# A gate table in pieces of 64 tokens, read for two expert groups at once, with its loads and the gelu loads at later places and the rows spread otherwise

## The chip, the core and the metric

The kernel runs on one core of a Trainium2 chip. The metric is the time of the whole program on the device in microseconds (us). Three runs of the kernel before took 2616.76 to 2627.11 us, with a median of 2618.74 us.

## What is computed

Two transformer blocks follow each other on 512 tokens of width 1024. The change touches the middle of the first block, a product-key expert layer with 16384 experts. Every token picks 16 experts for each of 8 heads, and an expert adds gate × gelu(down row · token) × up row:

```python
def peer_ffn(x, w_query, keys_1, keys_2, expert_down, expert_up):
    q = (x @ w_query).astype(f32).reshape(b, s, PEER_HEADS, 2, PEER_HALF)
    s1 = jnp.einsum("bshc,hkc->bshk", q[..., 0, :], keys_1)
    s2 = jnp.einsum("bshc,hkc->bshk", q[..., 1, :], keys_2)
    v1, i1 = lax.top_k(s1, PEER_TOPK)
    v2, i2 = lax.top_k(s2, PEER_TOPK)
    ...
    top_score, pos = lax.top_k(cand_score, PEER_TOPK)
    experts = jnp.take_along_axis(cand_idx, pos, axis=-1)
    gates = jax.nn.softmax(top_score, axis=-1)
    ...
        u = jnp.take(expert_down, ei, axis=0)
        act = jax.nn.gelu(jnp.einsum("btd,bthkd->bthk", xi, u), approximate=False)
        vv = jnp.take(expert_up, ei, axis=0)
        return jnp.einsum("bthk,bthkd->btd", gi * act, vv)
```

The numbers are float32; the kernel splits each factor of a large product into a high and a low half-precision part and multiplies three times.

## The kernel before

**Two ways for the experts.** The last 384 tokens (`TD`) go through all experts densely: the gelu of every expert for every token is formed and multiplied by a gate that is zero for experts that were not picked. The 16384 experts are 32 groups of 512, two groups make a pair `q` (16 pairs). The first 128 tokens are done row by row: 128 steps fetch one row of the down table for each token with an indirect DMA from GpSimd (`fetch`, 0.5 MB a step, a ring of 4 buffers), VectorE multiplies it with the token and sums (`row_step`, L1003), and 128 further steps do the same with the up table (L1015).

**Weights.** All weights stream through one list, 1 MB each. The SP queue loads a weight into one of 4 `raw` buffers (L304), ScalarE squares and sums it (`junk`, L319), TensorE adds that over the partitions (`ps_ss`, L206), VectorE and GpSimd make a power-of-two scale of it (`mi`, `scw`, L208 to L211), and ScalarE and VectorE split the weight into its high part (L333) and its low part (L334). Loads run three weights ahead of the one in use, the square and the sum three ahead, the split one ahead. A `raw` buffer is free after the split of its weight. All of it is in program order on each engine, so a `ps_ss` on TensorE that waits for a late load stops the matmuls behind it, though they don't need that weight yet.

**Stage 1** (about 700 to 1225 us of the trace) forms the gelu of the first 20 groups (`R1`), stores it in DRAM (`gedram`), selects the experts of the tokens (`select`), and writes the gate table into DRAM (`gdram`). `gate_chunk` makes the gates of 32 tokens: VectorE builds one-hot rows (`ohA`, `ohB`, `ohL`, `ohH`), TensorE multiplies them (`ps_g`), ScalarE copies the result into two staging tiles `stg`, one for each half of the experts, and issues their two writes of 1 MB. The pool has 3 `stg` buffers. `PLAN` orders the 12 chunks g0 to g11, the selections s1 to s3 and the down groups D.

**Stage 2** (about 1225 to 2083 us) runs over the pairs in the list `order` (0, 10, 1, 11, 2, 3, 12, 4, 5, 13, 6, 14, 7, 8, 15, 9). The list `stage2` holds its steps: `L` loads a pair's gelu back (two loads of 768 KB, 3 buffers), `D` forms a quarter of the gelu of a pair that has none yet, `C` (`combine`) multiplies gelu by gates (L1200) and splits the product into `cexp` (L1201 on ScalarE, L1202 on VectorE), and `U` multiplies a quarter of the pair's up weights with it (`ps_u`; 2 output tiles of 24 matmuls each, added into `hT` at L1223). `load_gates` reads the gates of one group, 768 KB in 12 runs of 512 bytes for each partition, into one of 2 `gt` buffers; it is called from `C` for the pair after. The quarters D of a later pair lie between the quarters U of an earlier one, so stretches with D alternate with stretches that have U alone and load stored gelu (the L stretches below: 1364 to 1444, 1520 to 1604, 1684 to 1744, 1797 to 1869 and 1950 to 2018 us).

**Rows.** `tick(n)` stands after each down or up tile and moves the row count on by n: `TK` holds n for a down tile in stage 2, an up tile beside down work, an up tile without it, a late and an early down tile of stage 1. What is left is done at the end of stage 2 in `rows_done`, before the last pair.

A scheduler merges these lists into one order for each engine and queue; the order is fixed when the program is built.

## Time and profile before

| | before |
|---|---|
| median of 3 runs | 2618.74 us |
| profiled execution, its own time | 2618.21 us |
| its span in the trace | 2616.3 us |
| TensorE busy | 2312.8 us (88%) |
| VectorE busy | 1820.9 us (70%) |
| ScalarE busy | 1352.1 us (52%) |
| GpSimd busy | 805.2 us (31%) |
| moved by DMA | 453.45 MB, mean 173 GB/s |

The page gives busy times of the whole span; what an edit is worth is read from the stretch in which it lies. A matmul is pipelined, so the mean duration of one is about twice the spacing at which they start, and the spacing is what counts. "PEclk" is the granted share of TensorE's full clock: 1.00 is 2.4 GHz and 0.50 is 1.2 GHz. The DMA share is the mean busy share of the 16 DMA engines.

### The profile page before, as it was taken

How to read it: one execution, taken by the hardware profiler on the slowest of the kernel's cores; microseconds unless marked ns; L12 is line 12 of the kernel's file. 1: busy time of each engine (PE TensorE's matmuls, PEld its weight loads, DVE VectorE, ACT ScalarE, POOL GpSimd, SP SyncE). 2: the span in 40 equal slices, each digit the busy share in tenths (PEclk: the TensorE clock that was granted, in tenths of full speed). 3: DMA queues.
4: the chain of work that ended last, by engine and by line, in shares of the span. 5: the costliest groups of instructions: out<-in, count | busy, mean ns of one | idle time of the engine just before them, and what ended most of it. 6: DMA issues, size and time to landing. Idle time of an engine off the chain costs nothing.

```text
span 2616.3 us, 37153 instructions
## 1 busy us (share of the span) xinstructions
PE 2312.8 (88%) x14242; PEld 1375.9 (53%) x14242; DVE 1820.9 (70%) x3865; ACT 1352.1 (52%) x1738; POOL 805.2 (31%) x782
## 2 busy tenths in 40 slices
PE   6999999989999988977797987979897769999997
PEld 2337896334655555644453554545454556555545
DVE  6877554386657798976786877788776853766555
ACT  6453223574655567766453634545453545454543
POOL 0002444020102344723564463657565420000000
PEclk9999999999999999988898998999998979999999
DMA  4220002342244547758988787788877724100121
GB/s 187 81 81 33 1 1 101 145 165 94 83 149 175 199 160 268 257 202 299 292 312 293 258 313 273 265 301 309 285 282 262 268 82 145 65 17 33 65 97 33
DMA packets 133075, 453.45 MB, mean 173 GB/s; under 512 B 9761, under 2 KB 61473, under 8 KB 102689
## 3 DMA queue, kind: packets, MB, share of 16 engines
q1 hardware_dynamic: 85872, 272.79, 30.2%
q0 software_dynamic: 36864, 134.23, 14.3%
q10 hardware_dynamic: 10160, 44.05, 4.3%
q8 instruction: 112, 1.84, 0.3%
q14 instruction: 67, 0.54, 0.1%
HBM read 408.05 MB, written 42.99 MB: 172 GB/s over the span
## 4 chain that ended last, share of the span: by engine, by line
PE 41%; DVE 24%; DMA 16%; ACT 9%; issue 7%; POOL 3%; ACTq 0%; POOLq 0%; DVEq 0%; SPq 0%
DVE sp L334 5%; PE ps_in L372 4%; PE ps_in L373 4%; PE ps_in L374 4%; DMA ring<-in_up_rows_dram,rowi 4%; DMA raw<-in_up_dram 3%; DMA ring<-in_down_rows_dram,rowi 3%; ACT junk L319 3%; ACT sp L333 2%; DMA raw<-in_down_dram 2%; PE ps_d L374 2%; DVE usp L334 2%; PE ps_d L373 2%; PE ps_d L372 2%; PE ps_r L572 2%
## 5 line engine op out<-in xcount | busy, mean ns | idle before, releaser
L319 ACT ACTIVATE junk<-raw 128x2048 bf16<-128x2048 f32 (+1 forms) x202 | 382.9, 1896 | 418.4 <-DMA raw<-in_up_dram 244.8
L334 DVE SCALAR_TENSOR_TENSOR sp<-raw,scw,sp 128x2048 f16<-128x2048 f32 (+2 forms) x140 | 326.6, 2333 | 122.2 <-ACT sp L333 122.1
L374 PE MATMUL ps_d<-xn,sp 128*128 128x384 f16 x1024 | 341.8, 336 | 39.0 <-DVE sp L334 39.0
L374 PEld LDWEIGHTS <-sp 128*128 128x128 f16 (+1 forms) x2320 | 230.8, 100 | 249.3 <-DVE sp L334 45.3
L372 PE MATMUL ps_d<-xn,sp 128*128 128x384 f16 x1024 | 344.0, 336 | 12.6 <-ACT sp L333 8.0
L374 PE MATMUL ps_u<-cexp,usp 128*128 128x384 f16 (+2 forms) x1024 | 340.6, 333 | 8.2 <-DVE usp L334 8.2
L372 PEld LDWEIGHTS <-sp 128*128 128x128 f16 (+1 forms) x2320 | 231.1, 100 | 215.3 <-issue 31.7
L373 PE MATMUL ps_d<-xn,sp 128*128 128x384 f16 x1024 | 343.7, 336 | 0.0
L373 PE MATMUL ps_u<-cexp,usp 128*128 128x384 bf16 (+2 forms) x1024 | 341.1, 334 | 2.7 <-DVE cexp L1202 2.7
L372 PE MATMUL ps_u<-cexp,usp 128*128 128x384 f16 (+2 forms) x1024 | 340.6, 334 | 2.7 <-ACT usp L333 2.7
L373 PEld LDWEIGHTS <-sp 128*128 128x128 f16 (+1 forms) x2320 | 230.9, 100 | 209.3 <-issue 39.9
L333 ACT ACTIVATE sp<-raw,scw 128x2048 f16<-128x2048 f32 (+2 forms) x140 | 276.9, 1980 | 74.5 <-DVE scw L210 31.6
L372 PE MATMUL ps_in<-xn,sp 128*128 128x512 f16 (+2 forms) x728 | 274.2, 378 | 5.8 <-DVE cv L499 3.3
L374 PE MATMUL ps_in<-xn,sp 128*128 128x512 f16 (+2 forms) x728 | 274.2, 378 | 0.4 <-DVE sp L334 0.4
L373 PE MATMUL ps_in<-xn,sp 128*128 128x512 f16 (+2 forms) x728 | 274.2, 378 | 0.0
L996 POOL DMA_INDIRECT ring<-in_down_rows_dram,rowi x128 | 186.0, 1453 | 233.1 <-DVE ring L1003 141.7
L996 POOL DMA_INDIRECT ring<-in_up_rows_dram,rowi x128 | 201.7, 1576 | 165.4 <-DVE ysum L1015 103.7
L1015 DVE SCALAR_TENSOR_TENSOR ysum<-ring,rowg,ysum 128x1024 f32<-128x1024 f32 x127 | 162.5, 1280 | 44.2 <-DMA ring<-in_up_rows_dram,rowi 43.8
L211 POOL TENSOR_SCALAR scw<-mi 128x1 int32<-128x1 int32 x136 | 81.5, 599 | 350.9 <-DVE mi L208 325.9
L1003 DVE SCALAR_TENSOR_TENSOR ring<-ring,xrow 128x1024 f32<-128x1024 f32 x128 | 155.3, 1220 | 40.4 <-DMA ring<-in_down_rows_dram,rowi 40.4
L333 ACT ACTIVATE usp<-raw,scw 128x2048 f16<-128x2048 f32 x62 | 123.8, 1997 | 98.8 <-PE ps_u L374 85.8
L206 PE MATMUL ps_ss<-ss,ones_b 128*128 128x1 bf16 x202 | 34.1, 169 | 147.8 <-ACT junk L319 89.3
(444 smaller groups left out, 4323.2 us busy)
## 6 DMA issues: line engine op xcount, KB each, us to landing
raw<-in_down_dram SPq DMA_DIRECT2D x64, 1024.0 KB, 5.4
raw<-in_up_dram SPq DMA_DIRECT2D x64, 1024.0 KB, 6.7
raw<-in_w_in_dram SPq DMA_DIRECT2D x45, 1024.0 KB, 4.8
gdram<-stg ACTq DMA_DIRECT2D x24, 1024.0 KB, 7.4
gt<-gdram SPq DMA_DIRECT2D x30, 768.0 KB, 9.2
gedram<-gelu ACTq DMA_DIRECT2D x20, 768.0 KB, 5.1
gelu<-gedram SPq DMA_DIRECT2D x20, 768.0 KB, 8.5
raw<-in_w_ada_dram SPq DMA_DIRECT2D x12, 1024.0 KB, 4.8
```

The costliest lines, as they stand in the source:

```text
L206: T.matmul(ps, ones_b, sb[:, 2 * u + 1:2 * u + 2], start=(u == 0), stop=(u == n - 1))
L211: side[0].tensor_scalar(sc[:, 1:2], mi, 1.0, float(50 << 23), op0=ALU.mult, op1=ALU.add)
L319: act(junk[:, :e["n"]], e["raw"][:, :e["n"]], AF.Square, accum_out=ss[:, j:j + 1])
L333: act(sp[:, 0, :n], e["raw"][:, :n], AF.Copy, scale=e["s"])
L334: rq["lo"] = V.scalar_tensor_tensor(sp[:, 1, :n], e["raw"][:, :n], e["s"], sp[:, 0, :n], op0=ALU.mult, op1=ALU.subtract)
L372: T.matmul(ps, wh, xh, start=start, stop=False)
L373: T.matmul(ps, wh, xl, start=False, stop=False)
L374: T.matmul(ps, wl, xh, start=False, stop=stop)
L572: T.matmul(pr[:, R4(r)], Tm[:, R4(r)], x[:, R4(r)], start=True, stop=True)
L996: G.indirect_dma_start(out=r, out_offset=None, in_=src, in_offset=bass.IndirectOffsetOnAxis(ap=rowi[s % P // 64][:, s % 64:s % 64 + 1], ax ...
L1003: V.scalar_tensor_tensor(r, r, 1.0, xrow, op0=ALU.mult, op1=ALU.mult, accum_out=rowu[:, s:s + 1])
L1015: V.scalar_tensor_tensor(ysum[0], r, g, ysum[0], op0=ALU.mult, op1=ALU.add)
```

## The change

Five edits:

- The gate table is written and read in pieces of 64 tokens (`TC`) and no longer 32. Two calls of `gate_chunk` fill one pair of `stg` tiles, which is written once, as 2 × 2 MB. There are 2 `stg` buffers of 16 KB a partition where there were 3 of 8 KB, and 10 slabs where there were 14. `select` takes one `stg` buffer for its three work tiles where it took three.
- `load_gates` reads the gates of a pair at once: 1.5 MB in 6 runs of 2 KB for each partition, into a single `gt` buffer of the size of the former two.
- In the list `stage2`, C of the next pair stands behind the first U of a pair (before: ahead of it), the gate load of the pair after it (`G`, a step of its own) behind the second U, and the gelu load behind the third. At the start, two of the four D quarters of the second pair stand behind the first C.
- `TK` changes from (1.9, 1.1, 0.9, 0.5, 0.8) to (2.0, 1.15, 0.95, 0.2, 1.0).
- gelu tiles have the layout of 6 × 4 × 64 where they had 12 × 4 × 32; the instructions on them keep their element counts.

```diff
-TK = (1.9, 1.1, 0.9, 0.5, 0.8)
+TK = (2.0, 1.15, 0.95, 0.2, 1.0)
...
-    stage2 = [("L", order[0])] + ([("L", order[1])] if early_(order[1]) else halves_(order[1])) + [("C", order[0])]
+    x = [("L", order[1])] if early_(order[1]) else halves_(order[1])
+    stage2 = [("L", order[0])] + x[:2] + [("C", order[0]), ("G", order[1])] + x[2:]
     for i, q in enumerate(order):
-        if i + 1 < 16:
-            stage2.append(("C", order[i + 1]))
-        if i + 2 < 16 and early_(order[i + 2]):
-            stage2.append(("L", order[i + 2]))
+        extra = [[("C", order[i + 1])] if i < 15 else [], [("G", order[i + 2])] if i < 14 else [],
+                 [("L", order[i + 2])] if i < 14 and early_(order[i + 2]) else [], []]
         for u in range(4):
-            stage2 += [("U", q, u)] + slots[i][u]
+            stage2 += [("U", q, u)] + extra[u] + slots[i][u]
...
     def gate_chunk(ch):
-        stg = [s1.tile([P, 64, 32], F32, tag="stg", name="stg", bufs=3) for _ in range(2)]
+        if ch % 2 == 0:
+            stg_[:] = [s1.tile([P, 64, TC], F32, tag="stg", name="stg", bufs=2) for _ in range(2)]
+        stg = stg_
...
-        for hf in range(2):
-            nc.scalar.dma_start(gd[ch, hf].rearrange("p i t -> p (i t)"), stg[hf].rearrange("p i t -> p (i t)"))
+        for hf in range(2 * (ch % 2)):
+            nc.scalar.dma_start(gd[ch // 2, hf].rearrange("p i t -> p (i t)"), stg[hf].rearrange("p i t -> p (i t)"))
...
-    def load_gates(g, q=nc.sync):
-        gt = pools["2"].tile([P, TD // 32, 4, 32], F32, tag="gt", name="gt", bufs=2)
-        hf, o = divmod(g * 4, 64)
-        q.dma_start(gt.rearrange("p c i t -> p c (i t)"), gd[:, hf, :, o:o + 4, :].rearrange("c p i t -> p c (i t)"))
-        gts[g] = gt
+    def load_gates(q, eng=nc.sync):
+        gt = pools["2"].tile([P, TD // TC, 8, TC], F32, tag="gt", name="gt", bufs=1)
+        hf, o = divmod(q * 8, 64)
+        eng.dma_start(gt.rearrange("p c i t -> p c (i t)"), gd[:, hf, :, o:o + 8, :].rearrange("c p i t -> p c (i t)"))
+        gts[q] = gt
```

How the scheduler's order moves is shown at four places. First ScalarE's order at the seam between the chunks g9 and g10 in stage 1. Before:

```order
L1143 COPY stg<-ps_g 128x4x64 x15
L1146 DMA gdram<-stg 128x2048 x2
L1143 COPY stg<-ps_g 128x4x64 x16
L1146 DMA gdram<-stg 128x2048 x2
L984 ACTIVATE gelu<-ps_d,dsc 128x12x32 x2
```

And now:

```order
L1151 DMA gdram<-stg 128x4096 x2
L1148 COPY stg<-ps_g 128x4x64 x4
L984 ACTIVATE gelu<-ps_d,dsc 128x6x64 x2
L1148 COPY stg<-ps_g 128x4x64 x4
L319 ACTIVATE junk,ss<-raw 128x2048
L1148 COPY stg<-ps_g 128x4x64 x8
```

The write ahead of the copies is twice as large, the copies behind it need both of its buffers, and the next write stands 32 copies on where it stood 16 on.

Second, ScalarE's order at the end of stage 1, from the last gate write on. Before:

```order
L1146 DMA gdram<-stg 128x2048 x2
L319 ACTIVATE junk,ss<-raw 128x2048
L1187 DMA gt<-gdram 128x12x128 x2
L333 ACTIVATE sp<-raw,scw 128x2048
L319 ACTIVATE junk,ss<-raw 128x2048
```

And now:

```order
L1151 DMA gdram<-stg 128x4096 x2
L333 ACTIVATE sp<-raw,scw 128x2048
L1192 DMA gt<-gdram 128x6x512
L319 ACTIVATE junk,ss<-raw 128x2048
L984 ACTIVATE gelu<-ps_d,dsc 128x6x64 x2
```

A split has moved ahead of the first gate load and a square behind it.

Third, VectorE's order at the same place, around the first two gate products (L1200 before, L1205 now). Before:

```order
L1194 TENSOR_REDUCE ca<-cs 128x1
L1200 SCALAR_TENSOR_TENSOR gelu<-gt,ca,gelu 128x1536 x2
L334 SCALAR_TENSOR_TENSOR sp<-raw,scw,sp 128x2048
L208 TENSOR_SCALAR mi<-ps_ss 128x1
L1003 SCALAR_TENSOR_TENSOR ring,rowu<-ring,xrow 128x1024
```

And now:

```order
L334 SCALAR_TENSOR_TENSOR sp<-raw,scw,sp 128x2048
L1003 SCALAR_TENSOR_TENSOR ring,rowu<-ring,xrow 128x1024 x4
L209 TENSOR_SCALAR mi<-ps_ss 128x1
L1205 SCALAR_TENSOR_TENSOR gelu<-gt,ca,gelu 128x1536
L211 TENSOR_SCALAR scw<-mi 128x1
L1205 SCALAR_TENSOR_TENSOR gelu<-gt,ca,gelu 128x1536
L334 SCALAR_TENSOR_TENSOR sp<-raw,scw,sp 128x2048
```

One split of a down weight and four row steps now stand ahead of the gate products.

Fourth, the SP queue in the second of the L stretches (each row is a load; 768 KB for a `gelu`, 768 KB for a `gt` before and 1.5 MB now, 1 MB for a `raw`). Before:

```order
L1187 DMA gt<-gdram 128x12x128
L1181 DMA gelu<-gedram 128x1536
L304 DMA raw<-in_up_dram 128x2048
L1187 DMA gt<-gdram 128x12x128
L1181 DMA gelu<-gedram 128x1536
L304 DMA raw<-in_up_dram 128x2048
L1187 DMA gt<-gdram 128x12x128 x2
L1181 DMA gelu<-gedram 128x1536
L304 DMA raw<-in_up_dram 128x2048
L1187 DMA gt<-gdram 128x12x128
```

And now:

```order
L1186 DMA gelu<-gedram 128x1536
L304 DMA raw<-in_up_dram 128x2048
L1186 DMA gelu<-gedram 128x1536
L304 DMA raw<-in_up_dram 128x2048
L1192 DMA gt<-gdram 128x6x512
L1186 DMA gelu<-gedram 128x1536
L304 DMA raw<-in_up_dram 128x2048
L1192 DMA gt<-gdram 128x6x512
L304 DMA raw<-in_up_dram 128x2048 x2
```

Ahead of the first two `raw` loads one load has gone, and gates come later in the stretch.

On VectorE, the gate products of this stretch stand so. Before, both groups of a pair together behind their preloaded gates:

```order
L1200 SCALAR_TENSOR_TENSOR gelu<-gt,ca,gelu 128x1536
L208 TENSOR_SCALAR mi<-ps_ss 128x1
L1200 SCALAR_TENSOR_TENSOR gelu<-gt,ca,gelu 128x1536
L210 TENSOR_SCALAR scw<-mi 128x1
L1223 SCALAR_TENSOR_TENSOR hT<-ps_u,yd,hT 128x384
```

And now, with the last product of one pair first and the first product of the next pair, for which the single `gt` buffer is loaded in between, nine rows on:

```order
L1205 SCALAR_TENSOR_TENSOR gelu<-gt,ca,gelu 128x1536
L209 TENSOR_SCALAR mi<-ps_ss 128x1
L1198 TENSOR_REDUCE ca<-cs 128x1
L1199 TENSOR_REDUCE ca<-cs 128x1
L211 TENSOR_SCALAR scw<-mi 128x1
L1229 SCALAR_TENSOR_TENSOR hT<-ps_u,yd,hT 128x384
L1003 SCALAR_TENSOR_TENSOR ring,rowu<-ring,xrow 128x1024
L1208 TENSOR_TENSOR cexp<-gelu,cexp 128x6x4x64
L1229 SCALAR_TENSOR_TENSOR hT<-ps_u,yd,hT 128x384
L1003 SCALAR_TENSOR_TENSOR ring,rowu<-ring,xrow 128x1024
L209 TENSOR_SCALAR mi<-ps_ss 128x1
L1205 SCALAR_TENSOR_TENSOR gelu<-gt,ca,gelu 128x1536
L334 SCALAR_TENSOR_TENSOR usp<-raw,scw,usp 128x2048
```

Two output tiles (`hT`) lie between the two gate products now, and a weight split stands right behind the second.

## Rows read from the trace of the kernel before

**Rows 1.** Busy times by stretch (us): stage 1's end, parts of stage 2; columns first.

```profile
core 0: us, PE busy (x) PEld busy (x) DVE busy (x) ACT busy (x) POOL busy (x), PEclk, DMA share, GB/s
900.00:1225.00 325.00, 281.46 (x2143) 180.39 (x2141) 284.54 (x756) 230.11 (x348) 147.06 (x130) 0.94 0.64 237
1225.00:1290.00 65.00, 31.18 (x143) 16.06 (x144) 39.24 (x56) 27.60 (x27) 31.88 (x29) 0.71 0.85 284
1364.00:1444.00 80.00, 61.62 (x347) 34.70 (x345) 55.48 (x84) 26.32 (x23) 40.00 (x38) 0.89 0.85 290
...
1950.00:2018.00 68.00, 53.44 (x298) 29.90 (x297) 51.07 (x57) 22.43 (x20) 42.07 (x38) 0.89 0.82 292
1290.00:2083.00 793.00, 686.38 (x4122) 402.73 (x4120) 608.49 (x737) 384.69 (x320) 429.10 (x398) 0.94 0.82 285
```

**Rows 2.** TensorE's waits in 1290 to 2083 us: total us, times, longest.

```profile
PE ps_ss L206 <- ACT junk L319: 54.8, 15, 10.5
PE ps_ss L206 <- DVE mi L208: 39.6, 18, 5.9
```

**Rows 3.** VectorE's waits in 1290 to 2083 us.

```profile
DVE ysum L1015 <- DMA ring<-in_up_rows_dram,rowi: 36.0, 16, 6.8
...
DVE ring L1003 <- DMA ring<-in_down_rows_dram,rowi: 28.9, 11, 4.4
...
DVE gelu L1200 <- DMA gelu<-gedram: 17.9, 5, 8.2
```

**Rows 4.** The chain that ended last, in 1416 to 1432 us: start, us, what.

```profile
1416.40 2.40 DVE usp L334
...
1418.82 10.94 DMA raw<-in_up_dram
...
1431.89 0.16 PE ps_ss L206
```

**Rows 5.** Busy by stretch: moving a gt, a gelu, weights and rows, then 2 KB runs.

```profile
1588.00:1592.00 4.00, 0.12 (x2) 0.12 (x2) 3.81 (x4) 2.00 (x2) 2.18 (x1) 0.50 0.63 175
1608.00:1612.00 4.00, 3.87 (x24) 2.22 (x23) 4.00 (x6) 3.98 (x4) 2.04 (x1) 1.00 0.58 197
...
2043.00:2048.00 5.00, 5.00 (x33) 3.01 (x31) 3.21 (x5) 1.49 (x1) 2.87 (x4) 1.00 0.81 297
...
2163.00:2170.00 7.00, 7.00 (x43) 4.08 (x42) 0.00 (x0) 3.24 (x6) 0.00 (x0) 1.00 0.93 306
```

**Rows 6.** ScalarE at the seam g9 to g10, in order of time.

```profile
1193.64 0.81 ACTq L1146 DMA_DIRECT2D gdram<-stg  x2
...
1198.70 1.96 ACT L1143 COPY stg<-ps_g 128x256 f32<-128x256 f32 x4 [3.54 <-DMA gdram<-stg]
```

**Rows 7.** The page's DMA issues: KB each, median us to landing.

```profile
gdram<-stg ACTq DMA_DIRECT2D x24, 1024.0 KB, 7.4
gt<-gdram SPq DMA_DIRECT2D x30, 768.0 KB, 9.2
```

**Rows 8.** VectorE's row steps by shape in 900 to 1225 us: busy, mean ns.

```profile
L1003 DVE SCALAR_TENSOR_TENSOR ring<-ring,xrow 128x1024 f32<-128x1024 f32 x26 | 31.7, 1220 | 0.0
```

**Rows 9.** TensorE's longest wait in 900 to 1225 us.

```profile
PE ps_d L374 <- DVE sp L334: 27.9, 9, 7.0
```

**Rows 10.** TensorE's waits in 1220 to 1290 us.

```profile
PE ps_d L374 <- DVE sp L334: 11.1, 1, 11.1
...
PE ps_d L372 <- ACT sp L333: 6.0, 1, 6.0
```

**Rows 11.** VectorE in order of time, the first gate product.

```profile
1238.41 1.82 DVE L1200 SCALAR_TENSOR_TENSOR gelu<-gt,ca,gelu 128x1536 f32<-128x1536 f32 x1 [11.71 <-DMA gt<-gdram]
```

**Rows 12.** The chain again, in 1220 to 1245 us.

```profile
1221.66 5.91 DMA gdram<-stg
...
1228.18 12.79 DMA gt<-gdram
```

**Rows 13.** Busy times at the end of stage 2, where rows alone run.

```profile
2083.00:2106.00 23.00, 1.30 (x8) 1.19 (x7) 14.62 (x22) 2.00 (x2) 8.93 (x8) 0.55 0.65 229
```

More of the change, by code (lines that the diff above doesn't have):

```diff
@@ L105 @@
 TD = 384
+TC = 64
 RING = 4
@@ L930, in tile_model @@
     s1 = stage1.enter_context(tc.tile_pool(name="stage1", bufs=1))
-    pools["s"] = stage1.enter_context(tc.tile_pool(name="slab2", bufs=14))
+    pools["s"] = stage1.enter_context(tc.tile_pool(name="slab2", bufs=10))
     keys = raw("keys").rearrange("p (j m) -> p j m", j=16)
@@ L964, in tile_model @@
     i1T, i2T, ghT, glT = (selT[:, i] for i in range(4))
-    gd = drp.tile([TD // 32, 2, P, 64, 32], F32, name="gdram")
+    gd = drp.tile([TD // TC, 2, P, 64, TC], F32, name="gdram")
     lim = [0]
@@ L972, in expert_down @@
             pool, n = (s1, 2) if g < R1 else (pools["2"], GB)
-            gelu[g] = pool.tile([P, TD // 32, 4, 32], F32, tag="gelu", name="gelu", bufs=n)
+            gelu[g] = pool.tile([P, TD // TC, 4, TC], F32, tag="gelu", name="gelu", bufs=n)
         t, e = gelu[g], need(("d", g, u))
@@ L983, in expert_down @@
             proj3(ps[:, :TD], e, c, xnd)
-            act(t[:, :, 2 * u + c], ps[:, :TD].rearrange("p (c t) -> p c t", t=32), AF.Gelu, scale=gs)
+            act(t[:, :, 2 * u + c], ps[:, :TD].rearrange("p (c t) -> p c t", t=TC), AF.Gelu, scale=gs)
             tick(TK[0] if g >= R1 else TK[3] if g >= nd else TK[4])
@@ L1086, in select @@
         p16, st, i1, i2 = (smp.tile([P, 16, nh], F16, tag=t, name=t, bufs=1) for t in ("p16", "st", "i1", "i2"))
-        ge, t1, t2 = (s1.tile([P, 64, 32], F32, tag="stg", name="stg", bufs=3).rearrange("p i t -> p (i t)")
-                      .bitcast(F16)[:, 0:256 * nh].rearrange("p (a k h) -> p a k h", a=16, k=16) for _ in range(3))
+        tmp = s1.tile([P, 64, TC], F32, tag="stg", name="stg", bufs=2).rearrange("p i t -> p (i t)").bitcast(F16)
+        ge, t1, t2 = (tmp[:, i * 256 * nh:(i + 1) * 256 * nh].rearrange("p (a k h) -> p a k h", a=16, k=16)
+                      for i in range(3))
         each = lambda t: t[:, None].to_broadcast([P, 16, 16, nh])
@@ L1121, in select @@
         V.scalar_tensor_tensor(glT[:, sl], ps[:, 0:P], GSC, ghT[:, sl], op0=ALU.mult, op1=ALU.subtract)
+    stg_ = []
     def gate_chunk(ch):
-        stg = [s1.tile([P, 64, 32], F32, tag="stg", name="stg", bufs=3) for _ in range(2)]
+        if ch % 2 == 0:
+            stg_[:] = [s1.tile([P, 64, TC], F32, tag="stg", name="stg", bufs=2) for _ in range(2)]
+        stg = stg_
         for o8 in range(4):
@@ L1140, in gate_chunk @@
                     T.matmul(ps[:, r * P:(r + 1) * P], B[:, q, :, e2], Al[:, q, :, e2], start=False, stop=True)
-                tl_ = o8 * 8 + q4 * 4
+                tl_ = ch % 2 * 32 + o8 * 8 + q4 * 4
                 for hf in range(2):
@@ L1179, in load_gelu @@
     def load_gelu(g):
-        t = pools["2"].tile([P, TD // 32, 4, 32], F32, tag="gelu", name="gelu", bufs=GB)
+        t = pools["2"].tile([P, TD // TC, 4, TC], F32, tag="gelu", name="gelu", bufs=GB)
         nc.sync.dma_start(t.rearrange("p c i t -> p (c i t)"), ged[g])
         gelu[g] = t
-    def load_gates(g, q=nc.sync):
-        gt = pools["2"].tile([P, TD // 32, 4, 32], F32, tag="gt", name="gt", bufs=2)
-        hf, o = divmod(g * 4, 64)
-        q.dma_start(gt.rearrange("p c i t -> p c (i t)"), gd[:, hf, :, o:o + 4, :].rearrange("c p i t -> p c (i t)"))
-        gts[g] = gt
+    def load_gates(q, eng=nc.sync):
[3 more added lines that the diff above has]
+        gts[q] = gt
     def combine(*gs):
@@ L1196, in combine @@
         for g in gs:
-            t, gt = gelu.pop(g), gts.pop(g)
+            t, gt = (v.rearrange("p c i t -> p c (i t)") for v in (gelu.pop(g), gts[g // 2][:, :, g % 2 * 4:g % 2 * 4 + 4]))
             ct = pools["2"].tile([P, 2, 4, TD], F16, tag="cexp", name="cexp", bufs=4)
-            hi, lo = (v.rearrange("p i (c t) -> p c i t", t=32) for v in (ct[:, 0], ct[:, 1].bitcast(BF16)))
+            hi, lo = (v.rearrange("p i (c t) -> p c i t", t=TC) for v in (ct[:, 0], ct[:, 1].bitcast(BF16)))
             V.scalar_tensor_tensor(t, gt, ca[:, 0:1], t, op0=ALU.mult, op1=ALU.mult)
+            t = t.rearrange("p c (i t) -> p c i t", i=4)
             nc.scalar.copy(hi, t)
@@ L1241, in tile_model @@
     pools["s"] = None
-    nU, lg = 0, [g for q in order for g in (2 * q, 2 * q + 1)]
-    for g in lg[:2]:
-        load_gates(g, nc.scalar)
+    load_gates(order[0], nc.scalar)
     lim[0] = 2 * P
@@ L1253, in tile_model @@
             combine(2 * x[1], 2 * x[1] + 1)
-            nU += 2
-            for g in lg[nU:nU + 2]:
-                load_gates(g)
+        elif x[0] == "G":
+            load_gates(x[1])
         elif x[1] != order[15]:
```

## The prediction

> **What bounds the kernel now.** I read the busy times by stretch first, then the waits of the engines in the stretches with idle, then the chain. In stage 1 TensorE is busy 281 of 325 us, and VectorE 285. In stage 2 the picture changes: the start (1225 to 1290) has TensorE busy 31 of 65 us, and the body (1290 to 2083) 686 of 793, with the DMA engines at a share of 0.82 [rows 1]. The 107 us of idle in the body are not spread evenly. The five stretches that load stored gelu (L stretches, 364 us in all, the first and the last shown) hold 77 of them, 21% of their time, at DMA shares of 0.82 to 0.91; the other 429 us hold 29, 7% [rows 1]. There TensorE stands at a `ps_ss` either because ScalarE's square came late, which waits for a weight to land (54.8 us), or because VectorE had not yet emptied the sum before it (39.6 us) [rows 2]. VectorE in turn stood waiting for rows (64.9 us) and for a stored gelu (17.9 us) [rows 3]. The chain shows how it hangs together: VectorE's split frees a buffer, the weight is issued at 1418.8 us and needs 10.9 us to land, and the `ps_ss` starts 2 us after that [rows 4]. So the body is bound by TensorE where DMA has room, and by DMA and by what stands in whose queue in the L stretches. Idle costs a little more than its own length: TensorE's granted clock is 0.89 over the two L stretches shown and 0.71 at the start, a mix of its levels 1.00 and 0.50 (2.4 and 1.2 GHz) [rows 1].
>
> **The change part by part.**
>
> *Longer runs in the gate loads.* Without company, a gate load moved 175 GB/s at a DMA share of 0.63, 278 GB/s for a full share; a gelu load 197 at 0.58, 340; weights and a row 297 at 0.81, 367; loads in runs of 2 KB 306 at 0.93, 329 [rows 5]. The 32 gate loads of 768 KB are 25.2 MB: 90.5 us of all DMA engines at 278 GB/s, 76.5 at 329. That gives back 14 us of DMA time, with ends of 0 (if 2 KB runs behave as 512-byte ones) and 22 (if as whole rows, at 367). This bears on a rule: the Trainium skill, "DMA: Bandwidth & Descriptors", section Specifications, puts the minimum transfer for line rate at 512 B. By it the old runs are already at full rate and the 14 us would be 0; the rates above disagree.
>
> *Rows moved.* By `TK`, stage 1 loses 52 late tiles × 0.3 and gains 16 early ones × 0.2: 12.4 row steps fewer. Stage 2 gains 48 down tiles × 0.1 and 120 up tiles × 0.05, 10.8 steps; 17.6 in place of 16 are left for the end. In stage 2 these 10.8 × 0.52 MB at 350 GB/s are 16 us of DMA time. So the two edits cancel over all of stage 2; in the L stretches, which have some 24 of the 32 gate loads and 4 of the new rows, they leave −10.5 + 6 = −4.5 us.
>
> *Stage 1.* The pieces hold the same bytes, but a write is 4 MB in place of 2 and no spare `stg` buffer is left. Copies stand right behind a write at g9 to g10, where ScalarE waited 3.5 us for the former write [rows 6]. One write of 1 MB landed after 7.4 us [rows 7], so I take that much more: 11 us. TensorE has 46 down and 32 gate matmuls before it needs ScalarE again, about 9 us less what has run by then: +7 us on the path, bounds 0 and 11. At g1 to g2 and g5 to g6 gelu activations at TensorE's pace stand ahead of the copies and cover most of the longer write: +1 us each. Selections still wait for one written buffer, as before. Against it, 11 to 12 row steps of 1.22 us leave VectorE [rows 8], 14 us, in a part where TensorE waits 27.9 us for VectorE's splits [rows 9]; VectorE is on the path a part of the time only, so −4, bounds 0 and −14. Sum +5.
>
> *Start of stage 2.* TensorE lost 6.0 us while ScalarE, waiting to issue the first gate load, could not split, and 11.1 us because VectorE, which had waited 11.7 us for the gates, held the next split behind them [rows 10, 11]. The write took 5.9 us and the load 12.8 [rows 12]. Now the write is twice as long (+5, if another 2 MB take about the 5.9 us of these), and the load, one in place of two, shorter by 2 to 4, so the gates come no sooner. But a split and four row steps of VectorE now stand ahead of the gate product, and the first product is needed after two quarters D, not four. Of the 17 us I take 10 back, bounds 0 (the longer write holds ScalarE longer, and D runs dry) and −17.
>
> *Body.* The L stretches: −4.5 us of DMA time, as above. The queue: at the second L stretch, two loads stood ahead of each of the first two weights, and one stands there now; gates come a weight or two later, and one more load falls into the stretch with D, which has room. A load of 0.79 MB at 340 GB/s is 2.3 us; two weights in each of five stretches, half of it on the path: −11. Stored gelu is asked for by VectorE one split later, so the 17.9 us of waits [rows 3] shrink, half of that on the path: −5. The new rows cost 1.22 us of VectorE and 1.5 us of DMA each in stretches that TensorE bounds: +3. Against all this stands a new wait, the first rival; for the forecast I take a third of it, +6. Sum −12, with ends of −45 (L stretches as little idle as the others: 364 × 0.14 = 51, less the rows) and +30.
>
> *End.* Some 16 rows run alone in 23 us [rows 13]; 1.6 more at 1.4 us each: +2. The instructions on the new layouts keep their element counts, and I take their durations as unchanged; each 0.1 us on the 192 copies into `stg` would be 19 us of ScalarE, at most half of that on the path.
>
> Sum: 5 − 10 − 12 + 2 = −15. The profiled execution took 2618.2 us, within 0.6 of the median of the runs. Forecast: 2603 us.
>
> **The rivals.**
>
> *VectorE waits for its own gates (slower).* With one `gt` buffer, the load for a pair starts after the last product of the pair before, and the first product of the new pair stands two output tiles later in VectorE's order: 48 matmuls at 0.16 us, 8 us. The load is twice as large. A gate load of 768 KB took 9.2 us in the median [rows 7]; 0.79 MB more at 329 GB/s makes it 11.6. That leaves 4 us or more at two places in each of five L stretches, 40 us or more of VectorE, and a weight split, which frees the next `raw` buffer, stands right behind the product. For it: the rows already show how VectorE's waits reach TensorE. Against it: VectorE waits for TensorE there as well, so the 8 us are often more. Should three quarters of it reach TensorE, +30 in place of +6, and the queue terms vanish (+16): 2618 + 5 − 10 + 30 − 4.5 + 3 + 2 = 2643. It decides where the load takes over 10 us from issue.
>
> *DMA stays the bound (no change).* The L stretches need the same bytes plus rows, and the order of queues only moves the idle about. Body 0, start −6: 2618 + 5 − 6 + 2 = 2619.
>
> *512 bytes are already full rate (no change).* Then the 10.5 us in the L stretches are not won, and new rows cost 6: body −1.5 in place of −12, which gives 2614. That is what the rule of the page cited above would make of it.
>
> *The L stretches become like the others (a larger gain).* Loads are spread, weights land in time, body −45: 2618 + 5 − 10 − 45 + 2 = 2570.
>
> **How the numbers follow.** The forecast, 2592 to 2614 by its own bounds, gets 0.45; VectorE's wait 0.18; DMA as the bound 0.14; full rate at 512 bytes 0.07; the larger gain 0.16. A half percent is 13 us and about what a measurement of this kernel can tell from no change, so faster means below 2605.6. Two thirds of the forecast's chance and all of the larger gain lie there: 0.30 + 0.16 = 0.46. No change gets 0.15 + 0.14 + 0.07 = 0.36. Slower, above 2631.8, gets 0.18. The range from 2572 to 2640 leaves out about half of the larger gain and half of VectorE's wait.
>
> **What would show it.** In the profile after: at g9 to g10 ScalarE's copies wait some 11 us for the write; TensorE is busy 40 us or so of the 65 behind the last gate write; the waits of `ps_ss` for the square in the L stretches fall below 54.8 us; the DMA time of the gate loads falls from some 90 us to 77. It is wrong if VectorE shows waits for `gt` of more than 20 us in the body, if the stage 1 copies got slower, or if the five L stretches are as idle as before.

## The result: 0.6% slower

The changed kernel took 2635.68 us in the median of 5 runs (2633.71 to 2643.43), the kernel before 2618.74. The ratio is 1.0061, with a 95% interval from 1.0033 to 1.0089: 17 us slower where 15 us faster was forecast. The range (2572 to 2640) holds the time; the sign is wrong.

The profiled execution has a span of 2633.9 us (2616.3 before). Four events that both traces have split the difference. Their times are starts and ends of single instructions, in us:

| | before | after | difference | forecast |
|---|---|---|---|---|
| last copy into `stg` (end of stage 1) | 1221.6 | 1226.9 | +5.3 | +5 |
| from there to the first up matmul (start of stage 2) | 53.9 | 45.2 | −8.7 | −10 |
| from there to the 120th add into `hT` (body) | 787.5 | 806.5 | +19.0 | −12 |
| from there to the end | 553.3 | 555.3 | +2.0 | +2 |

Three of four terms came as forecast, at least as sums. The body is off by 31 us, and with it the sign.

### The profile page after: what moved, and what is told of

Same layout as the page of the kernel before. It is cut to its first block, busy times and chain, and to the rows that moved or that the text cites. A ratio compares the mean times of both kernels' runs of the same rounds, so it can differ in the third digit from the quotient of the medians.

```text
span 2633.9 us, 37071 instructions
## 1 busy us (share of the span) xinstructions
PE 2315.7 (88%) x14242; PEld 1379.7 (52%) x14242; DVE 1821.3 (69%) x3865; ACT 1350.5 (51%) x1738; POOL 815.4 (31%) x782
## 4 chain that ended last, share of the span: by engine, by line
PE 40%; DMA 20%; DVE 18%; ACT 11%; issue 7%; POOL 3%; POOLq 0%; SPq 0%; DVEq 0%; ACTq 0%
PE ps_in L372 4%; PE ps_in L373 4%; PE ps_in L374 4%; DMA raw<-in_down_dram 4%; DMA ring<-in_up_rows_dram,rowi 4%; DVE sp L334 4%; ACT junk L319 3%; DMA raw<-in_up_dram 3%; DMA gt<-gdram 3%; ACT stg L1148 3%; DMA gdram<-stg 2%; DMA ring<-in_down_rows_dram,rowi 2%; ACT sp L333 2%; PE ps_d L374 2%; DVE usp L334 2%
## 5 line engine op out<-in xcount | busy, mean ns | idle before, releaser
L374 PE MATMUL ps_u<-cexp,usp 128*128 128x384 f16 (+2 forms) x1024 | 345.0, 338 | 24.6 <-DVE scw L211 24.3
L372 PE MATMUL ps_u<-cexp,usp 128*128 128x384 f16 (+2 forms) x1024 | 346.3, 339 | 1.4 <-ACT usp L333 1.4
L996 POOL DMA_INDIRECT ring<-in_down_rows_dram,rowi x128 | 197.1, 1540 | 197.6 <-DVE ring L1003 120.5
L996 POOL DMA_INDIRECT ring<-in_up_rows_dram,rowi x128 | 194.5, 1519 | 141.6 <-DVE ysum L1015 88.6
L372 PEld LDWEIGHTS <-usp 128*128 128x128 f16 x1024 | 105.4, 103 | 115.1 <-issue 58.2
```

Source lines behind the costliest of these rows:

```text
L372: T.matmul(ps, wh, xh, start=start, stop=False)
L374: T.matmul(ps, wl, xh, start=False, stop=stop)
L996: G.indirect_dma_start(out=r, out_offset=None, in_=src, in_offset=bass.IndirectOffsetOnAxis(ap=rowi[s % P // 64][:, s % 64:s % 64 + 1], ax ...
```

## The profile after

Busy times by stretch of the changed kernel (us, busy time of each engine with its instructions, granted clock, DMA share, GB/s): 65 us of the start, and the body from the first up matmul on.

```profile
1235.00:1300.00 65.00, 42.86 (x225) 23.18 (x224) 37.56 (x54) 29.77 (x28) 31.39 (x26) 0.83 0.84 308
1272.00:2078.60 806.60, 678.76 (x3978) 392.50 (x3976) 619.91 (x764) 383.94 (x322) 473.76 (x413) 0.94 0.82 289
```

And the body of the kernel before, between the same two events:

```profile
1275.50:2063.00 787.50, 674.59 (x3955) 390.39 (x3953) 603.85 (x734) 378.82 (x318) 429.92 (x399) 0.93 0.82 285
```

The start came out as the prediction's last part asked: TensorE is busy 42.9 of 65 us behind the last gate write ("40 or so"; 31 before [rows 1]). In the body TensorE has the same work, but its idle time rose from 113 to 128 us at the same DMA share of 0.82. VectorE is busy 16 us longer: the body holds 209 row steps now and held 195. The five L stretches (1368 to 1447, 1522 to 1612, 1692 to 1750, 1809 to 1881 and 1968 to 2033 us now) are as idle as before, 81 of 364 us for 77; the prediction named that as a sign that it is wrong.

The waits in 1290 to 2100 us of the changed kernel, TensorE's first and then VectorE's (total us, times, longest):

```profile
PE ps_ss L207 <- ACT junk L319: 65.8, 25, 8.3
PE ps_ss L207 <- DVE mi L209: 33.1, 16, 6.5
PE ps_u L374 <- DVE scw L211: 24.3, 4, 7.8
...
DVE ysum L1015 <- DMA ring<-in_up_rows_dram,rowi: 45.7, 20, 5.3
DVE ring L1003 <- DMA ring<-in_down_rows_dram,rowi: 33.5, 12, 4.8
DVE gelu L1205 <- DMA gt<-gdram: 32.9, 8, 5.3
```

TensorE waits 11 us more for squares that wait for weights (54.8 before [rows 2]), where the prediction asked for less, and 24.3 us at four up tiles for splits that VectorE did late. The last of TensorE's lines names `scw`, a step of 0.14 us that VectorE runs right behind each of these four splits. The same wait in the kernel before, in 1290 to 2083 us:

```profile
PE ps_u L374 <- DVE usp L334: 8.2, 4, 4.4
```

VectorE waits 14 us more for rows, and 32.9 us for gates. That last row did not exist in the body before; in return its 17.9 us for stored gelu [rows 3] are gone. The prediction named a wait for `gt` of more than 20 us as the sign of its slower rival. VectorE's instructions on the gates in one L stretch show the mechanism (start, us, what, idle before and its releaser):

```profile
1408.41 1.81 DVE L1205 SCALAR_TENSOR_TENSOR gelu<-gt,ca,gelu 128x1536 f32<-128x1536 f32 x1
...
1425.26 3.54 DVE L1205 SCALAR_TENSOR_TENSOR gelu<-gt,ca,gelu 128x1536 f32<-128x1536 f32 x2 [2.84 <-DMA gt<-gdram]
...
1440.01 1.82 DVE L1205 SCALAR_TENSOR_TENSOR gelu<-gt,ca,gelu 128x1536 f32<-128x1536 f32 x1 [4.90 <-DMA gt<-gdram]
```

The product at 1408 is the last of a pair. The load for the next pair goes out behind it and the products run at 1425; the next load goes out behind those, and the product at 1440 waits again. So the obvious reading of this profile is that the single gate buffer ate the gain. The experiments below don't bear that out.

At the seam g9 to g10 ScalarE's copies waited for the longer write in two pieces, 9.1 us together (11 forecast; 3.5 before [rows 6]):

```profile
1204.30 1.94 ACT L1148 COPY stg<-ps_g 128x256 f32<-128x256 f32 x4 [6.61 <-DMA gdram<-stg]
1209.52 1.97 ACT L1148 COPY stg<-ps_g 128x256 f32<-128x256 f32 x4 [2.45 <-DMA gdram<-stg]
```

From 900 us to the end of stage 1 the copies waited 24.7 us for writes, at six places; before it was 8.0 us at three.

**The packets of the gate loads.** The profile's page counts DMA time by queue only. The packet records of the same traces show more, since the gate loads have packets of a size of their own in stage 2. Before: 49152 packets of 512 bytes, median 27 ns, mean 31.7, 97.5 us for each of the 16 DMA engines. After: 12288 packets of 2 KB, median 84 ns, mean 115.8, 88.9 us. By the medians 2 KB went from 108 to 84 ns, 22% less; by the means from 127 to 116, 9% less. What came between is a tail: packets of over twice the median held 14% of the gate loads' time before and 32% after. I call this share the **long packets**. The gelu, weight and row packets hardly changed (weights 362 and 356 ns).

## The experiments

Two theories stood at the start. *Theory 1*: the single gate buffer makes VectorE wait. *Theory 2*: loads placed later and rows moved cost the time. A third came out of the first four runs: *the table's layout in DRAM*. A partition's row is 64 experts × 64 tokens × 4 bytes = 16 KB now, where it was 8 KB, so the 128 partitions of a load read from addresses at a distance of 16 KB. A second distance grew with it. A partition reads one run from each chunk of tokens, and the runs lie 256 rows apart (two halves of 128 partitions): 4 MB now, 2 MB before. Every run below that changes the layout changes both distances by the same factor. Where the text gives the distance of the rows, it names the layout by it; which of the two distances costs the time isn't shown.

All ratios are to the kernel before, run on the same chip. "Body" and "packets" (time of the gate packets for each DMA engine) are of the one profiled execution; the runs of one kernel lie 0.2 to 1.3% apart, so the ratio decides.

| run | ratio (95% interval) | last `stg` copy | body | packets | long packets |
|---|---|---|---|---|---|
| kernel before | 1 | 1221.6 | 787.5 | 97.5 | 14% |
| changed kernel | 1.0061 (1.0033 to 1.0089) | 1226.9 | 806.5 | 88.9 | 32% |
| after_noread | 1.0012 (0.9991 to 1.0033) | 1228.3 | 800.4 | 77.9 | 18% |
| after_gt1k | 1.0160 (1.0125 to 1.0195) | 1229.0 | 829.0 | 103.8 | 38% |
| after_tk0 | 1.0002 (0.9981 to 1.0023) | 1234.6 | 796.3 | 86.2 | 29% |
| pieces64 | 1.0090 (1.0055 to 1.0125) | 1232.7 | 809.7 | 103.8 | 38% |
| before_tk1 | 1.0055 (1.0029 to 1.0081) | 1225.7 | 806.0 | 99.7 | 17% |
| before_order | 1.0052 (1.0029 to 1.0075) | 1221.5 | 805.4 | 97.0 | 14% |
| after_pad | 0.9969 (0.9945 to 0.9994) | 1230.3 | 774.5 | 72.0 | 11% |
| pieces64_pad | 0.9925 (0.9909 to 0.9942) | 1232.1 | 769.4 | 79.2 | 11% |
| before_pitch16 | 1.0093 (1.0059 to 1.0126) | 1219.1 | 815.0 | 106.0 | 24% |
| before_pad | 0.9881 (0.9817 to 0.9945) | 1218.9 | 770.1 | 92.5 | 3% |
| after_tk0_pad | 0.9899 (0.9871 to 0.9928) | 1235.1 | 779.0 | 71.8 | 11% |
| p64pad_start | 0.9864 (0.9831 to 0.9897) | 1229.7 | 759.1 | 79.9 | 12% |
| gt1k_pad | 0.9971 (0.9952 to 0.9991) | 1228.2 | 782.2 | 78.3 | 10% |
| before_order_pad | 0.9907 (0.9875 to 0.9940) | 1223.3 | 772.5 | 92.1 | 3% |
| before_pad_start | 0.9888 (0.9859 to 0.9917) | 1219.5 | 771.7 | 92.8 | 3% |

### Taking away the wait for gates

```diff
-            V.scalar_tensor_tensor(t, gt, ca[:, 0:1], t, op0=ALU.mult, op1=ALU.mult)
+            V.scalar_tensor_tensor(t, t, ca[:, 0:1], t, op0=ALU.mult, op1=ALU.mult)
```

> The changed kernel, with its gate products reading the gelu in the place of the gates (gelu times scale times gelu). All gate loads are still issued and move the same bytes, but no product waits for one and none holds the gate buffer; the output is not that of the reference. Theory 1 (VectorE waits for its own gates, because one buffer serves all pairs): the 33 us of VectorE's waits for gates behind 1290 us vanish, the body shortens by 15 to 25 us, and the time is 2610 to 2620 us. Theory 2 (the loads placed later and the rows moved are what costs the time): the time stays within 5 us of the changed kernel, 2631 to 2641 us.

The product takes the gelu twice and leaves the gates out. Measured: 1.0012, some 13 us faster than the changed kernel, between what the two theories gave. But the run did more than was meant. With no product that holds the buffer, all 16 gate loads ran ahead and were issued between 1239 and 1441 us, so the stretches behind had none. And the idle time came back at another place. TensorE's waits in the body of this run:

```profile
PE ps_ss L207 <- ACT junk L319: 86.4, 27, 10.4
PE ps_ss L207 <- DVE mi L209: 31.6, 16, 5.9
PE ps_u L374 <- DVE usp L334: 3.4, 2, 2.2
```

The 24 us for VectorE's splits are gone, and the wait for weights is 21 us longer. The run shows that the wait for gates can be removed without TensorE gaining as much; it doesn't tell the theories apart.

The other way to take the wait away keeps the loads where they are, in two halves with a buffer each:

```diff
-        gt = pools["2"].tile([P, TD // TC, 8, TC], F32, tag="gt", name="gt", bufs=1)
+        for g in (2 * q, 2 * q + 1):
+            gt = pools["2"].tile([P, TD // TC, 4, TC], F32, tag="gt", name="gt", bufs=2)
...
```

> The changed kernel with the gates of a pair loaded as two halves of 768 KB, each into a buffer of its own (6 runs of 1 KB a partition; the same SBUF in all, the same place in the order). A half's load now starts after the product of the same half of the pair before, and is half as long. Theory 1: most of the wait goes, VectorE waits less than 12 us for gates in the body, and the time is 2612 to 2622 us. Theory 2: within 5 us of the changed kernel.

Measured: 1.0160, 26 us *slower* than the changed kernel, outside of both theories. VectorE's wait for gates in the body fell from 32.9 to 7.9 us, as theory 1 wanted. But the halves also cut the runs to 1 KB, so the wait was not removed alone: what rose is the packets' time. Runs of 1 KB took 103.8 us, more than the 97.5 of twice as many runs of 512 bytes, with 38% in long packets.

### Rows and order

```diff
-TK = (2.0, 1.15, 0.95, 0.2, 1.0)
+TK = (1.9, 1.1, 0.9, 0.5, 0.8)
```

> The changed kernel with the row counts of the kernel before (1.9, 1.1, 0.9, 0.5, 0.8). Theory 1: the waits for gates stay, and the time is within 5 us of the changed kernel. Theory 2, rows as its cause: the 11 rows more in stage 2 cost 1.5 us each, so the time falls by 10 to 16 us, to 2620 to 2626 us.

The same edit the other way round in the kernel before:

> The kernel before with the row counts of the changed kernel alone (2.0, 1.15, 0.95, 0.2, 1.0). As the prediction had it: stage 1 gains some 4 us, the body loses 3, the end 2: 2614 to 2624 us. As the changed kernel with the old counts suggests (15 us faster than with the new ones): the body of stage 2 pays about 2 us for each of 11 rows more and more for the loads pushed late, stage 1 gives back 5 to 10, so 2625 to 2635 us.

Measured: the old counts bring the changed kernel back to 1.0002, 15 us; the new counts alone cost the kernel before 0.55%, 14 us. Both agree, and the prediction had this edit at +7 (−4 in stage 1, +6 of DMA time in the L stretches, +3 in the body, +2 at the end). The body of before_tk1 is 18 us longer, for 11 rows more: 1.7 us each, near the 1.5 us that their 0.52 MB take at 350 GB/s. Its line, to be read beside that of the kernel before:

```profile
1277.40:2083.40 806.00, 675.03 (x3955) 390.14 (x3953) 616.62 (x757) 380.13 (x318) 443.26 (x410) 0.93 0.82 286
```

In after_tk0 VectorE waits even longer for gates in the body than in the changed kernel (32.9 us), and the kernel is as fast as the one before:

```profile
DVE gelu L1205 <- DMA gt<-gdram: 44.0, 8, 9.5
```

For the order, `stage2` of the changed kernel was put into the kernel before:

> The kernel before with the changed kernel's list of steps in stage 2 alone: C behind the first U, the gate loads behind the second, the gelu loads behind the third, two D quarters of the second pair behind the first C. Pieces of 32 tokens, two gate buffers of 768 KB and the row counts stay. As the prediction had it: the start gives back 10 us and the queue 10 to 16: 2590 to 2605 us. If loads that come later cost as much as they free: 2612 to 2625 us. If the place is what costs the changed kernel its time: over 2630 us.

The edit is the one shown with the change, with `G` loading both groups:

```diff
-            nU += 2
-            for g in lg[nU:nU + 2]:
-                load_gates(g)
+        elif x[0] == "G":
+            load_gates(2 * x[1])
+            load_gates(2 * x[1] + 1)
```

Measured: 1.0052, 14 us slower, the last of the three cases. The first up matmul does come 5 us earlier (1270.2 for 1275.5). The five L stretches, by the starts of the same `ps_ss`, are some 7 us shorter together, and the stretches with D 22 us longer. These sums are good to about 5 us, since marks move in the order too; their signs are clear. The body also holds 199 row steps where it held 195, some 7 us of this at the 1.7 us above.

### The layout of the table

The first hint was a run that should have been the control: the changed kernel with `TK` and `stage2` as before and the two gate buffers of after_gt1k, so that only the pieces of 64 tokens are left of the change.

> The changed kernel's pieces of 64 tokens with two staging buffers in stage 1, but the order of stage 2, the row counts and two gate buffers of 768 KB as in the kernel before (runs of 1 KB). Both theories: the body of stage 2 is that of before or up to 10 us shorter by the longer runs; stage 1 ends 5 to 12 us later by the longer writes (forecast +7 without the rows). The time is 2613 to 2628 us.

Measured: 1.0090, out of the range. Stage 1 ended 11 us later, as expected. But the body took 22 us longer than before, and on SP, VectorE and ScalarE its instructions stand in the order of the kernel before but for a few at the start. What differed was the gate loads: 103.8 us of packets. The next runs changed nothing but the layout in DRAM, by unused places for experts.

```diff
-    gd = drp.tile([TD // TC, 2, P, 64, TC], F32, name="gdram")
+    gd = drp.tile([TD // TC, 2, P, 66, TC], F32, name="gdram")
...
-            nc.scalar.dma_start(gd[ch // 2, hf].rearrange("p i t -> p (i t)"), stg[hf].rearrange("p i t -> p (i t)"))
+            nc.scalar.dma_start(gd[ch // 2, hf, :, 0:64].rearrange("p i t -> p (i t)"), stg[hf].rearrange("p i t -> p (i t)"))
```

> The changed kernel with the gate table in DRAM padded from 64 to 66 experts, so that the rows of the partitions lie 16.5 KB apart and no longer 16 KB; sizes of all transfers stay. In the trace of the changed kernel 32% of the time of the gate loads' packets lies in packets of over twice their median of 84 ns (14% before, at 512 bytes and 8 KB apart). If the distance is the cause: that share falls under 20%, the packets' time from 89 us to 72 to 78 us a DMA engine, and the time by 6 to 15 us, to 2620 to 2630 us. If the long packets come from other traffic: within 5 us of the changed kernel.

> The run pieces64 (old order, old row counts, two gate buffers of 768 KB, runs of 1 KB) with the same padding to 66 experts. Its body of stage 2 has the order of the kernel before and took some 22 us longer, with 38% of the gate packets' time in packets of over twice their median. If the distance of 16 KB between partitions is the cause: the body comes back to within 6 us of the kernel before, and the time falls to 2622 to 2632 us. If not: 2641 to 2652 us.

Measured: 0.9969 and 0.9925, that is 24 us and 43 us off by 512 bytes of padding a row (128 KB more between the runs of a partition), in both more than was expected. The long packets fell to 11% in both, the packets' time from 88.9 to 72.0 and from 103.8 to 79.2 us. The body of after_pad, between the same events:

```profile
1275.70:2050.30 774.60, 669.22 (x3978) 389.07 (x3976) 618.79 (x764) 380.61 (x318) 478.18 (x413) 0.95 0.83 300
```

300 GB/s at a share of 0.83, where the changed kernel had 289 at 0.82: the DMA engines are as busy and move more. VectorE still waits for gates as long as in the changed kernel, and now the kernel is faster than the one before (without padding):

```profile
DVE gelu L1205 <- DMA gt<-gdram: 29.9, 8, 7.3
```

To separate the layout from the length of a run, the kernel before got the distance of 16 KB (128 places for experts, 64 used; the diff), and in another run 8.5 KB (68 places):

```diff
-    gd = drp.tile([TD // 32, 2, P, 64, 32], F32, name="gdram")
+    gd = drp.tile([TD // 32, 2, P, 128, 32], F32, name="gdram")
```

> The kernel before with its gate table spread in DRAM so that the partitions' rows lie 16 KB apart (128 places for experts, 64 used) in the place of 8 KB; runs of 512 bytes and all sizes stay. If the distance of 16 KB alone makes the long packets: their share of the gate packets' time rises from 14% to over 25%, the packets' time from 97.5 to 105 us or more, and the time by 8 to 20 us, to 2628 to 2640 us. If only longer runs collide at that distance: within 5 us of the kernel before.

> The kernel before with its gate table padded from 64 to 68 experts, so that the rows of the partitions lie 8.5 KB apart in the place of 8 KB. If a distance of 8 KB costs something too: the share of the packets over twice the median falls from 14% to about 11%, the packets' time by 3 us, and the time by 2 to 6 us, to 2613 to 2618 us. If 512-byte runs at 8 KB don't collide: within 2 us of the kernel before.

Measured: 1.0093 and 0.9881. The layout alone, with the runs and the order of the kernel before, makes 24 us more or 31 us less. The second was far more than expected: the packets' time fell by only 5 us an engine, but the long packets went from 14% to 3%. The body of before_pad:

```profile
1266.90:2037.10 770.20, 670.21 (x3955) 388.89 (x3953) 604.33 (x734) 380.31 (x318) 433.43 (x400) 0.94 0.84 293
```

Gates, stored gelu and rows landed earlier with it; the weights hardly moved (6.7 to 6.6 us and 7.0 to 7.3). The DMA issues in 1290 to 2083 us (count, KB each, median us to landing), for the kernel before:

```profile
raw<-in_up_dram SPq DMA_DIRECT2D x59, 1024.0 KB, 6.7
gt<-gdram SPq DMA_DIRECT2D x27, 768.0 KB, 9.4
raw<-in_down_dram SPq DMA_DIRECT2D x19, 1024.0 KB, 7.0
gelu<-gedram SPq DMA_DIRECT2D x17, 768.0 KB, 9.5
...
ring<-in_up_rows_dram,rowi POOLq DMA_INDIRECT x122, 7.4
```

for before_pitch16:

```profile
raw<-in_up_dram SPq DMA_DIRECT2D x59, 1024.0 KB, 7.3
gt<-gdram SPq DMA_DIRECT2D x27, 768.0 KB, 10.6
raw<-in_down_dram SPq DMA_DIRECT2D x19, 1024.0 KB, 6.4
gelu<-gedram SPq DMA_DIRECT2D x17, 768.0 KB, 9.7
ring<-in_up_rows_dram,rowi POOLq DMA_INDIRECT x114, 8.1
```

and for before_pad:

```profile
raw<-in_up_dram SPq DMA_DIRECT2D x59, 1024.0 KB, 6.6
gt<-gdram SPq DMA_DIRECT2D x27, 768.0 KB, 8.1
raw<-in_down_dram SPq DMA_DIRECT2D x19, 1024.0 KB, 7.3
gelu<-gedram SPq DMA_DIRECT2D x16, 768.0 KB, 7.1
...
ring<-in_up_rows_dram,rowi POOLq DMA_INDIRECT x128, 6.8
```

Rows and gelu, whose own packets take about the same time in the three kernels, land at other times as the gate table's layout changes (rows 7.4, 8.1 and 6.8 us, gelu 9.5, 9.7 and 7.1). A reading of this, not shown: the packets of a load are spread over engines that also carry the gate loads, and one engine with long packets holds up the whole load. The packet records don't name the engine.

The table's writes bear on which distance counts. They have the rows of the partitions at the same distances, but a single run for each partition, and no more than 1% of their packets' time is long in any of these kernels (a packet of 8 KB takes 317 ns in the mean with rows 8 KB apart, 322 with 16 KB). That fits the distance between a partition's runs better, but writes in runs of 8 KB are no test of reads in runs of 512 bytes.

### What is left with the padding

Three runs combine edits that are shown above with the padding: the changed kernel with the old row counts, the changed kernel with two gate buffers, and the kernel before with the changed order.

> The changed kernel with the old row counts and the table padded to 66 experts. The padding gave the changed kernel 24 us and the old row counts 15; if the two add up, 2594 to 2602 us. If both take the same idle time, about 2605 to 2612 us, no better than one of them.

> The changed kernel with the gates of a pair as two halves of 768 KB in two buffers (runs of 1 KB) and the table padded to 66 experts. Against after_pad (2615 us, ratio 0.9969, one buffer, VectorE waits 30 us for gates in the body) it has no wait for a buffer of a whole pair but 7 us more of packet time (79 for 72 us). If the single buffer is what costs: 0.985 to 0.992 of the kernel before. If VectorE's wait is cover for other waits and DMA time is what counts: 0.997 to 1.003.

> The kernel before with the changed kernel's list of steps alone (before_order: ratio 1.0052) and the table padded to 68 experts (before_pad: 0.9881). If the later loads cost by themselves: 0.991 to 0.996. If they only cost together with the slow gate loads: 0.985 to 0.990, no worse than before_pad.

Measured: after_tk0_pad 0.9899, so padding and old row counts add up (18 us between it and after_pad): the rows cost what they did. gt1k_pad 0.9971, the same as after_pad: VectorE's wait for gates fell from 29.9 to 3.5 us against 6 us more of packets, and nothing moved. So the two offset each other within the intervals; what either is worth alone isn't shown. before_order_pad 0.9907 against before_pad 0.9881, between the two ranges expected and with intervals that overlap: a cost of the later places isn't shown here, and the wide interval of before_pad can't exclude one.

The table holds one more comparison. Padded on both sides, the change still makes the kernel slower: after_pad 0.9969 against before_pad 0.9881, 23 us. And with either layout the row counts make up the difference: with the old counts the changed kernel isn't told apart from the kernel before, without padding (1.0002) or with it (0.9899 against 0.9881). So the layout costs both kernels time and padding helps both; there is no sign that it makes the one slower than the other.

Two runs looked for a kernel that beats both. The edit is the same in each, on pieces64_pad and on before_pad: two D quarters of the second pair stand behind the first C (here on before_pad).

```diff
-    stage2 = [("L", order[0])] + ([("L", order[1])] if early_(order[1]) else halves_(order[1])) + [("C", order[0])]
+    x = [("L", order[1])] if early_(order[1]) else halves_(order[1])
+    stage2 = [("L", order[0])] + x[:2] + [("C", order[0])] + x[2:]
```

> The run pieces64_pad (old order and row counts, two gate buffers, runs of 1 KB, padding to 66 experts: 2604 us) with the changed kernel's start of stage 2 alone (two D quarters of the second pair behind the first C). The order alone brought the first up matmul forward by 5 us in before_order. If that is kept to the end: 2596 to 2601 us. If the body takes it back, as it did there: 2602 to 2607 us.

> before_pad with the changed kernel's start of stage 2 alone: two D quarters of the second pair behind the first C. The first up matmul comes 5 us earlier. If the start is kept to the end, as in p64pad_start: 0.983 to 0.987 of the kernel before. If the body takes it back: 0.988 to 0.990.

Measured: 0.9864 (2589.85 us) and 0.9888 (2592.34 us). The first is the fastest kernel found, 1.4% below the kernel before. It isn't told apart from before_pad (0.9881), which changes one number and one slice of the kernel before. The start's gain is kept in the one and isn't seen in the other.

## Why the prediction was wrong

**Where the 32 us went.** Two of the runs lie on the way from the kernel before to the changed one, so the way has three steps: to before_order (1.0052), from there to after_tk0, which adds the pieces, the longer runs and the single buffer (1.0002), and from there to the changed kernel, which adds the row counts (1.0061). In us, with the prediction's terms for the same edits:

| | forecast | measured |
|---|---|---|
| list of steps (start −10, queue −11, gelu −5) | −26 | +14 |
| pieces, longer runs, single buffer (stage 1 +9, DMA −10.5, new wait +6) | +4.5 | −13 |
| row counts (−4, +6, +3, +2) | +7 | +15 |

Each measured step is good to some 6 to 9 us, and another order of the edits would split them otherwise. The step that failed most is the first: loads at later places were to free the L stretches at no cost elsewhere. The rows were forecast at half of what they cost. The layout, which the prediction passed over, changes in the second step, which gained time all the same.

**Stage 1 (+5 forecast, +5.3).** Right in the sum and in what it named: the copies waited 9.1 us at the seam. Its parts were mis-sized against each other. Pieces of 64 tokens with the old counts moved the last copy by 11 to 13 us (pieces64, after_tk0; forecast 9), and the rows taken out gave back some 8 in the changed kernel (4 forecast); in before_tk1, without the longer writes, nothing came back (+4).

**Start (−10, −8.7).** Right, with its mechanism. VectorE waited 15.5 us for the gates (11.7 before [rows 11]), but the split and the row steps now stand ahead of that wait. TensorE's wait for VectorE's splits went from 11.1 to 6.4 us and its 6.0 us for ScalarE's are gone [rows 10]. As a part of the time it was worth little, though: before_order had the start's gain and lost more behind it.

**Longer runs (14 us of DMA time, 8.6).** This term was mis-sized: the gate loads went from 97.5 to 88.9 us, where 90.5 to 76.5 was forecast. The prediction took 329 GB/s for a full share from weights that are read in runs of 2 KB elsewhere in the trace [rows 5] and so held a rate to be a property of the run's length. In the quiet case it is: the medians follow 8 ns a packet and 0.037 ns a byte from 512 bytes (27 ns) to 8 KB (309), and the median 2 KB of gates got 22% cheaper, which also contradicts the rival of full rate at 512 bytes. But the change also moved the partitions' rows from 8 to 16 KB apart, and a partition's runs from 2 to 4 MB, which the diff says in one line (`TC` in the shape of `gd`) and the prediction passed over. after_pad has the time that the step forecast, and more (72.0 us). But less packet time did not give a faster kernel: after_tk0_pad has 71.8 us where before_pad has 92.5, and the two aren't told apart (0.9899 and 0.9881); in the former stage 1 ends 16 us later, the start is 8 us shorter and the body 9 us longer.

The Trainium skill, "DMA: Bandwidth & Descriptors", section Latency and other measured facts, has a rule that spoke against this change: copies slow down when the rows of the partitions lie at large powers of two in HBM, by its table from 2 MB on (164 GB/s there, 207 at 512 KB), and padding by 4 KB cures it while 192 bytes do not; the mechanism is called an inference. The runs here agree in kind: both plain layouts were slower than their padded ones. Which distance is at work they don't show: the rows of the partitions, of which the rule speaks, lie 8 and 16 KB apart here, far below its table, and the runs of one partition 2 and 4 MB. Padding of 512 bytes a row, 128 KB between runs, was enough. The prediction should have weighed it.

**Rows (+7 in the sum, +15).** This term was mis-sized. The prediction let 16 us of DMA time for new rows cancel the 14 us from longer runs, charged 6 us to the L stretches and 3 to the others, and took 4 back in stage 1. Measured in before_tk1, the body pays 18 us: some 5 in the L stretches and 13 in the others, by the starts of the same `ps_ss`. The stretches with D had idle TensorE time of 7% [rows 1], and that was read as room; it was not room for another 0.5 MB.

**The queue and the gelu (−11 and −5).** This step failed, for the same reason. The later places did shorten the L stretches in before_order (−7) and lengthened the others (+22), where the prediction had put the moved loads at no cost because those stretches have room. The waits for stored gelu went as said, and bought nothing. With the padded table a cost of the later places isn't shown (before_order_pad), so part of the 14 us may come only together with the layout.

**End (+2, +2.0).** The agreement is luck: with the old row counts throughout, this stretch took 548 to 558 us in the runs above.

**The rival that came true in the trace.** VectorE waits for its own gates, 32.9 us in the body, and it decides where it was said to: a pair's load took 10.6 us in the median from issue to its last packet. Its time (2643) was nearer than the forecast. As the cause of the loss it isn't borne out: after_tk0 waits longer for gates (44.0 us) and is as fast as the kernel before, and with the wait taken away and the loads kept in place the kernel was slower (after_gt1k) or the same (gt1k_pad), though with more packet time in both. No run removed the wait alone, so what it costs by itself stays open. That VectorE waits for gates where it would otherwise wait for something else that DMA brings late is a reading.

The edits don't add up as single terms. Alone and without padding, pieces of 64 tokens in runs of 1 KB cost 24 us, the order 14 and the rows 14; together with runs of 2 KB they cost 17. The rows are the one term that costs much the same everywhere: 14 and 15 us, and 18 with padding.

## What to carry to other kernels

When a change alters the shape of a table in DRAM, look at the distances in DRAM between the partitions' rows and between a partition's runs as well as at the length of a run, and try a padded table first: it is an edit of one number. Pad the kernel before as well, or a gain of the padding passes for one of the change. Take packets by their median and their tail: in before_pad gelu and rows landed earlier when the tail of the gate loads went. And a wait that the profile names (VectorE for its gates) is a cause only if the time falls when it alone is removed; in after_noread another wait took its place.

## What was not expected of the hardware

- With 128 partitions' rows 16 KB apart in place of 8 KB (and a partition's runs 4 MB apart in place of 2), the same loads of 512-byte runs took 9% more packet time (106.0 for 97.5 us) and the kernel 0.9% longer; rows at 8.5 KB made it 1.2% faster. At 8 KB the cost was already there, unseen in the kernel before.
- At 16 KB, runs of 1 KB were slower by the byte (67.6 ns in the mean) than runs of 512 bytes at 8 KB (2 × 31.7 ns); at 16.5 KB they took 51.6 ns.
- The sum of the packets' time did not show the damage: 5 us of 97.5 went, and 31 us of the kernel's time.
